# Beginning the products of two later recurrence units in the opening of a hybrid decoder trunk

## The chip, the cores and the metric

The kernel runs on one core of a Trainium2 chip, in one launch. The metric is the device time of that launch in microseconds (us). All shares, spans and waits below are from one execution that the hardware profiler recorded.

## The reference

Two layers over a stream of 256 tokens of width 2048, conditioned on a vector c. The first layer has two kinds of heads that share one input projection; the second has another linear attention. Cut to what matters here, the mixer of the first layer:

```python
def hgrn2_fox_mixer(h, w_in, w_out, lower_bound, a_out_gain, q_gain, k_gain, f_bias):
    proj = h @ w_in
    ...
    qa, fa, ia, ga, qb, kb, vb, gb, fb = jnp.split(proj, cuts, axis=-1)
    z = split_heads(fa, A_HEADS).astype(jnp.float32)
    ...
    o_a = chunk_gated_linear_recurrence(jax.nn.silu(split_heads(qa, A_HEADS)), key,
                                        split_heads(ia, A_HEADS), log_forget)
    o_a = rms_norm(o_a, a_out_gain[:, None, :])
    o_a = merge_heads(o_a).astype(h.dtype) * jax.nn.silu(ga)
    ...
    o_b = forgetting_attention(q, k, split_heads(vb, B_HEADS), log_f)
    o_b = merge_heads(o_b).astype(h.dtype) * jax.nn.sigmoid(gb)
    return jnp.concatenate([o_a, o_b], axis=-1) @ w_out
```

The input h is the normalised stream, shifted and scaled by vectors that are products of silu(c) with a matrix `mod_w`. All of it is float32.

## The kernel before

**Products.** A product is 256 tokens by 1024 columns over 2048 rows of a weight matrix, or 16 k tiles of 128 rows. To keep float32 accuracy both operands are split into a rounded high half and the rest: ScalarE casts the weights to `hi` (L167), VectorE takes `lo = raw - hi` (L169), and TensorE makes three matmuls of 128x512 for each block (L190 to L192: hi·hi, hi·lo, lo·hi). A load brings 1 MiB, which is two *pieces* of two k tiles for one product of 512 columns; a piece is 12 matmuls. A product's sum (`acc`, 128 x 2 x 512) lies in one of the two buffers of the PSUM pool `pp`.

**Units.** The first layer's projection is cut into four recurrence units A0 to A3 and four attention units B0 to B3, each of two heads and two products (A20, A21 and so on). The products of A0 and A1 are made in the opening, the others in the body.

**The opening** (`start()`, L962 to L1135) is an order written out by hand. For each of 16 k tiles SP issues three loads of 1 MiB: two column tiles of `mod_w` (L984) and one tile of `start_w` (L989), which holds the 2048 columns of A0 and A1. VectorE sums the two column tiles (L109), ScalarE and VectorE make that k tile's operand hT (L1015 to L1017), and TensorE does 24 matmuls (L1031 to L1033), or, for the k tiles in `PLAIN`, 8 float32 matmuls without splitting (L1026). Three raw weight tiles, four `hi` and four `lo` buffers go round.

**The body** (`drive()`, L222) walks a list of pieces: first A2, A3, then B0 to B3, then the output projection O0 and what follows. Between pieces it issues steps of *jobs*. A job is a unit's recurrence (`hgrn_scores`: exponents ex, decays dec, products kd, scores sc, the state st; `hgrn_output`: output po, its squares oj, o) or its attention. `TICKS` gives each job a number of pieces within which it is to be done, and `finish` forces what is left before the next unit of its kind goes on. Column sums for later modulation (L109) are spread over the pieces at a rate for each product. From this program a scheduler fixes each engine's order, and the buffer that each tile gets; on the chip every engine runs its list strictly in order. An attention unit's second product is read by the copy of v (L792) and by the gate g_B: three functions on ScalarE (L294 to L296) and L794 on VectorE, which releases the sum's buffer.

Of the kernel before, what the change touches and what calls it, by code (L numbers as in the profile page):

```python
# [7 lines left out]
F32 = mybir.dt.float32  # L8
# [16 lines left out]
PLAIN = (0, 3, 6, 9, 12, 15)  # L25
# [6 lines left out]
TICKS = dict(hgrn0=12, hgrn1=19, hgrn=14, fox_gates=6, fox_probs=6, fox_out=6,  # L32
# [34 lines left out]
def build(tc, ctx, a, out):  # L67
# [74 lines left out]
    def add(name, w, act, done, before=None, rate=0.0, first=False, last=False):  # L142
        p = Product(name, w, act, done, before, rate)
        p.first, p.last = first, last
        pieces.extend((p, k) for k in range(2 * len(w)))
# [31 lines left out]
    def multiply(i, tiles=(0, 1)):  # L177
# [5 lines left out]
        for kk in range(2):  # L183
# [3 lines left out]
            for t in tiles:  # L187
                a_hi, a_lo = p.act(kt, t)
                o = p.ps[:, t, :]
                nc.tensor.matmul(o, a_hi, w_hi, start=(kt == 0), stop=False)  # L190
# [771 lines left out]
    def start():  # L962
# [15 lines left out]
        def fetch_columns(kt):  # L978
            for part in (1, 0):
                if (2 * kt + 1 - part) % 3 == 2:  # L980
# [6 lines left out]
        def fetch_weights(kt):  # L987
            raw_w[kt] = rawp.tile([P, 2048], F32, tag="raw", name=f"raw_s{kt}")
            nc.sync.dma_start(out=raw_w[kt], in_=a["start_w"][kt])  # L989
# [12 lines left out]
        def weights(kt):  # L1002
            if kt in PLAIN:
                return None
            return [split_weights(raw_w[kt][:, n * 1024:(n + 1) * 1024], f"s{kt}_{n}") for n in range(2)]
# [13 lines left out]
        def products(kt, ws, ns):  # L1019

            for n in ns:
                sl = slice((n % 2) * 512, (n % 2 + 1) * 512)
                for t in range(2):
                    o = acc[n][t]
                    if ws is None:
                        nc.tensor.matmul(o, tms[kt][:, t * P:(t + 1) * P], raw_w[kt][:, n * 512:(n + 1) * 512],  # L1026
                                         start=(kt == 0), stop=(kt == KT - 1))
                        continue
# [4 lines left out]
                    nc.tensor.matmul(o, a_lo, hi[:, sl], start=False, stop=(kt == KT - 1))  # L1033
# [21 lines left out]
        acc = {}  # L1055
        env["pp"] = ctx.enter_context(tc.tile_pool(name="pp", bufs=2, space=PSUM))
        for u in range(2):
            big = acc["qg", u] = env["pp"].tile([P, 2, 512], F32, tag="pp", name=f"acc_s{u}")
            acc[2 * u + 1] = [big[:, t] for t in range(2)]
# [30 lines left out]
        for u in range(2):  # L1090
            acc[2 * u] = [ps_mix(f"acc_s{u}_{t}") for t in range(2)]
# [3 lines left out]
        operand(1)  # L1095
        fetch_columns(2)
        for kt in range(1, KT):
            if kt + 2 < KT:
                fetch_columns(kt + 2)
            if kt + 1 < KT:  # L1100
                fetch_weights(kt + 1)
                columns(kt + 1)
            if kt == 3:
                nc.scalar.preload_act_table_set(SILU)
            ws = weights(kt)
            if kt + 1 < KT:
                operand(kt + 1)
            products(kt, ws, (1, 3, 0, 2))
# [20 lines left out]
    def after_start(acc, qg):  # L1129
# [4 lines left out]
        for u in range(2):  # L1134
            env["last", u] = job(hgrn_scores(u, 0) + hgrn_scores(u, 1) + hgrn_output(u), TICKS[f"hgrn{u}"])  # L1135


    def done_hgrn(u, half):
        def done(ps):
            if half == 0:  # L1140
                finish(env["last", u - 2])
                urgent.extend(hgrn_gates(u, [(slice(0, 2), ps)]))
            else:
                assert not urgent
                env["A", u]["qg"] = hgrn_silu(u, ps)
                env["last", u] = job(hgrn_scores(u, 0) + hgrn_scores(u, 1) + hgrn_output(u), TICKS["hgrn"])
        return done

    def done_fox(u, half):
        def done(ps):  # L1150
            if half == 0:
                finish(env["last", u + 2])
# [4 lines left out]
            else:  # L1157
                fox_values(u, ps)
                env["last", u + 4] = job(fox_output(u) + ([lambda: end_mix("out_b")] if u == 3 else []), TICKS["fox_out"])
# [136 lines left out]
    for u in (2, 3):  # L1296
        for half in range(2):
            add(f"A{u}{half}", quads(a["ab_w_in"][2 * u + half]), now_act, done_hgrn(u, half), rate=RATES["A"])
    for u in range(4):
        for half in range(2):  # L1300
# [58 lines left out]
def _layout(i):  # L1359
# [18 lines left out]
    s = np.stack([w[:, g] for g in groups[:4]])  # L1378
# [40 lines left out]
```

## Time and profile before

| | us |
|---|---|
| median of 3 runs | 2499.93 (2498.66 to 2501.02) |
| the profiled execution | 2495.23 |
| its span, first to last instruction | 2493.50 |
| TensorE (PE) busy | 2442.0 (98%) |
| VectorE (DVE) busy | 1772.8 (71%) |
| ScalarE (ACT) busy | 1168.8 (47%) |

The mean granted clock of TensorE is 0.997. A group's row gives line, engine, operation, output and inputs, shapes and count, then busy time and the mean of one in ns, then the idle time before it and what ended that. A wait's row gives the engine and work that waited, what it waited for, the total, the number of times and the longest. In the chain each row is start, length and work.

### The profile page before, as it was taken

What the parts mean: (1) busy time and instruction counts of PE and PEld (TensorE: products, weight loads), DVE (VectorE), ACT (ScalarE), POOL (GpSimd) and SP (SyncE); (2) the same over time, 40 slices, a digit from 0 to 9 for tenths busy, and PEclk for the clock granted to TensorE, in tenths of its full rate; (3) what the DMA queues carried; (4) which work ended last, traced back from release to release, by engine and by line L of the source; (5) the groups of instructions that cost most, each with busy time, mean ns of one, the idle gap of its engine ahead of it and who ended that gap; (6) DMA issues with size and microseconds to landing.
All of it is one profiled execution on the core that took longest, in us unless ns stands there. A gap on an engine that the chain in (4) does not pass through costs nothing.

```text
span 2493.5 us, 28661 instructions
## 1 busy us (share of the span) xinstructions
PE 2442.0 (98%) x11204; PEld 2002.5 (80%) x11204; DVE 1772.8 (71%) x2039; ACT 1168.8 (47%) x1625; POOL 89.6 (4%) x176
## 2 busy tenths in 40 slices
PE   7899999999999999999999999999999999999999
PEld 4578887887888888888888888888888888888887
DVE  6967887887788767767767787876776554644555
ACT  4255555545434444344345666654544344344343
POOL 0000000000000000000000000000000000000000
PEclk9999999999999999999999999999999999999999
DMA  9964767985798877777786667677486555555554
GB/s 390 420 258 168 286 253 290 347 320 215 288 367 339 318 285 285 289 286 283 286 292 208 236 246 248 250 280 260 175 313 237 188 195 189 188 191 193 190 189 148
DMA packets 93849, 647.48 MB, mean 260 GB/s; under 512 B 10417, under 2 KB 10993, under 8 KB 16401
## 3 DMA queue, kind: packets, MB, share of 16 engines
q1 hardware_dynamic: 70290, 476.59, 52.4%
q0 software_dynamic: 23424, 169.07, 18.2%
q8 instruction: 87, 1.43, 0.2%
q14 instruction: 48, 0.39, 0.0%
HBM read 641.39 MB, written 4.23 MB: 259 GB/s over the span
## 4 chain that ended last, share of the span: by engine, by line
PE 93%; DVE 4%; DMA 2%; ACT 1%; issue 1%; SPq 0%; ACTq 0%
PE acc_F L192 13%; PE acc_F L190 13%; PE acc_F L191 13%; PE acc_G L190 6%; PE acc_G L192 6%; PE acc_G L191 6%; PE acc_C L192 4%; PE acc_C L190 4%; PE acc_C L191 4%; PE acc_B L190 2%; PE acc_B L192 2%; PE acc_B L191 2%; PE acc_O L190 2%; PE acc_O L192 2%; PE acc_O L191 2%; DMA raw_s<-in_start_w_dram 2%
## 5 line engine op out<-in xcount | busy, mean ns | idle before, releaser
L169 DVE TENSOR_TENSOR lo<-raw_F,hi 128x1024 fp32r<-128x1024 f32 x352 | 429.5, 1223 | 302.3 <-ACT hi L167 302.1
L167 ACT CAST hi<-raw_F 128x1024 fp32r<-128x1024 f32 x352 | 370.6, 1054 | 478.1 <-PE acc_F L192 433.2
L192 PE MATMUL acc_F<-hi,hT_f 128*128 128x512 f32 x1408 | 551.1, 391 | 1.4 <-DVE hT_f L357 1.4
L190 PE MATMUL acc_F<-hi,hT_f 128*128 128x512 f32 x1408 | 548.7, 390 | 1.8 <-ACT hT_f L356 1.8
L191 PE MATMUL acc_F<-lo,hT_f 128*128 128x512 f32 x1408 | 548.4, 390 | 0.0
L109 DVE SCALAR_TENSOR_TENSOR mod<-mod,silu_c 128x2048 f32<-128x2048 f32 x160 | 365.3, 2284 | 4.2 <-DMA mod<-in_mod_w_dram 4.2
L169 DVE TENSOR_TENSOR lo<-raw_G,hi 128x1024 fp32r<-128x1024 f32 x176 | 214.2, 1222 | 139.3 <-ACT hi L167 139.1
L167 ACT CAST hi<-raw_G 128x1024 fp32r<-128x1024 f32 x176 | 185.4, 1055 | 268.5 <-PE acc_G L192 227.3
L192 PEld LDWEIGHTS acc_F<-hi,hT_f 128*128 128x128 f32 x1408 | 264.4, 188 | 56.9 <-DVE hT_f L357 3.0
L190 PEld LDWEIGHTS acc_F<-hi,hT_f 128*128 128x128 f32 x1408 | 264.5, 188 | 55.8 <-ACT hT_f L356 2.2
L191 PEld LDWEIGHTS acc_F<-lo,hT_f 128*128 128x128 f32 x1408 | 264.3, 188 | 55.1
L190 PE MATMUL acc_G<-hi,ct_f 128*128 128x512 f32 x704 | 273.5, 389 | 1.6 <-DVE res_G L405 1.6
L192 PE MATMUL acc_G<-hi,ct_f 128*128 128x512 f32 x704 | 274.4, 390 | 0.0
L191 PE MATMUL acc_G<-lo,ct_f 128*128 128x512 f32 x704 | 273.7, 389 | 0.0
L190 PEld LDWEIGHTS acc_G<-hi,ct_f 128*128 128x128 f32 x704 | 132.2, 188 | 29.6 <-DVE res_G L405 2.4
L191 PEld LDWEIGHTS acc_G<-lo,ct_f 128*128 128x128 f32 x704 | 132.2, 188 | 27.4
L192 PEld LDWEIGHTS acc_G<-hi,ct_f 128*128 128x128 f32 x704 | 132.2, 188 | 27.2
L190 PE MATMUL acc_C<-hi,hT_n 128*128 128x512 f32 x384 | 152.4, 399 | 0.9 <-ACT hT_n L356 0.9
L192 PE MATMUL acc_C<-hi,hT_n 128*128 128x512 f32 x384 | 151.3, 394 | 0.7 <-DVE hT_n L357 0.7
L191 PE MATMUL acc_C<-lo,hT_n 128*128 128x512 f32 x384 | 151.7, 395 | 0.0
L104 POOL DMA_DIRECT2D mod<-in_mod_w_dram x160 | 84.5, 528 | 1612.8 <-DVE mod L109 1449.8
L169 DVE TENSOR_TENSOR lo<-raw_C,hi 128x1024 fp32r<-128x1024 f32 x96 | 116.1, 1220 | 35.2 <-ACT hi L167 34.8
(343 smaller groups left out, 3399.7 us busy)
## 6 DMA issues: line engine op xcount, KB each, us to landing
raw_F<-in_ffn_w_in_dram SPq DMA_DIRECT2D x176, 1024.0 KB, 4.9
mod<-in_mod_w_dram POOLq DMA_DIRECT2D x160, 1024.0 KB, 5.2
raw_G<-in_ffn_w_out_dram SPq DMA_DIRECT2D x88, 1024.0 KB, 4.9
raw_C<-in_gla_w_in_dram SPq DMA_DIRECT2D x48, 1024.0 KB, 5.6
mod_s<-in_mod_w_dram SPq DMA_DIRECT2D x32, 1024.0 KB, 17.0
raw_B<-in_ab_w_in_dram SPq DMA_DIRECT2D x32, 1024.0 KB, 6.6
raw_s<-in_start_w_dram SPq DMA_DIRECT2D x16, 1024.0 KB, 13.9
raw_A<-in_ab_w_in_dram SPq DMA_DIRECT2D x16, 1024.0 KB, 5.0
```

The source lines that it names most:

```text
L104: nc.gpsimd.dma_start(out=tile, in_=a["mod_w"][l, part * KT + j])
L109: nc.vector.scalar_tensor_tensor(tile, tile, 1.0, silu_c, ALU.mult, ALU.mult, accum_out=modc[l, part][:, j:j + 1])
L167: nc.scalar.copy(out=hi, in_=w)
L169: env["lo"] = nc.vector.tensor_tensor(lo, w, hi, ALU.subtract)
L190: nc.tensor.matmul(o, a_hi, w_hi, start=(kt == 0), stop=False)
L191: nc.tensor.matmul(o, a_hi, w_lo, start=False, stop=False)
L192: nc.tensor.matmul(o, a_lo, w_hi, start=False, stop=(kt == last))
```

## The change

The opening gets four steps ahead of its 16: ("e", 0) to ("e", 3) multiply the first four k tiles with the 2048 columns of A2 and A3, from a new array `early_w` of 4 MiB, into the sums that A0 and A1 use afterwards. Eight ScalarE copies of 128x512 take these partial sums to two tiles in SBUF, and the accumulators are allotted anew. The column sums of k tiles 0 to 3 go with the four new steps, so steps s0 to s3 have none. The plain steps are now five of twenty: e0, s5, s8, s11 and s15 (before: 0, 3, 6, 9, 12 and 15 of sixteen). The column tiles of part 0 always take the two `modraw` buffers, those of part 1 the pool `h`; before, one in three took `modraw`.

In the body the products of A2 and A3 begin at their third piece, and a VectorE add puts the saved sums on (once for each of four products). Their order is A0 A1 B0 A2 B1 A3 B2 B3, and `finish` goes by the unit two places ahead in that order. The deadlines of A0 and A1 go from 12 to 9 and from 19 to 16.

```diff
-PLAIN = (0, 3, 6, 9, 12, 15)
+EARLY = 4
+PLAIN = (("e", 0), ("s", 5), ("s", 8), ("s", 11), ("s", 15))
+ORDER_AB = (("A", 0), ("A", 1), ("B", 0), ("A", 2), ("B", 1), ("A", 3), ("B", 2), ("B", 3))
...
-TICKS = dict(hgrn0=12, hgrn1=19, hgrn=14, fox_gates=6, fox_probs=6, fox_out=6,
+TICKS = dict(hgrn0=9, hgrn1=16, hgrn=14, fox_gates=6, fox_probs=6, fox_out=6,
...
-        pieces.extend((p, k) for k in range(2 * len(w)))
+        p.begin = begin
+        pieces.extend((p, k) for k in range(begin, 2 * len(w)))
...
-                if (2 * kt + 1 - part) % 3 == 2:
+                if part == 0:
                     tl = rawp.tile([P, D], F32, tag="modraw", name=f"mod_s{part}_{kt}", bufs=2)
...
+        steps = [("e", kt) for kt in range(EARLY)] + [("s", kt) for kt in range(KT)]
+        new = [kt if g == "e" or kt >= EARLY else None for g, kt in steps]
...
+        for i in range(len(steps)):
+            if i + 2 < len(steps) and i > 0 and new[i + 2] is not None:
+                fetch_columns(new[i + 2])
+            if i + 1 < len(steps):
+                if i > 0:
+                    fetch_weights(i + 1)
+                if i > 0 and new[i + 1] is not None:
+                    columns(new[i + 1])
...
+            if i > 0:
+                products(i, ws, (1, 3, 0, 2))
+            if i == EARLY - 1:
+                for u in range(2):
+                    early[u] = hpool.tile([P, 2, 2, 512], F32, tag="h", name=f"early_{u}")
+                for half in (1, 0):
+                    for u in range(2):
+                        for t in range(2):
+                            nc.scalar.copy(out=early[u][:, half, t], in_=acc[2 * u + half][t])
+                wide("s")
+                narrow("s")
...
     def done_hgrn(u, half):
         def done(ps):
+            nc.vector.tensor_tensor(ps, ps, env["early"][u - 2][:, half], ALU.add)
             if half == 0:
-                finish(env["last", u - 2])
+                finish(env["last", before_last("A", u)])
...
-    for u in (2, 3):
+    for kind, u in ORDER_AB[2:]:
         for half in range(2):
-            add(f"A{u}{half}", quads(a["ab_w_in"][2 * u + half]), now_act, done_hgrn(u, half), rate=RATES["A"])
-    for u in range(4):
-        for half in range(2):
+            if kind == "A":
+                add(f"A{u}{half}", quads(a["ab_w_in"][2 * u + half]), now_act, done_hgrn(u, half), rate=RATES["A"], begin=EARLY // 2)
+                continue
```

Three places where the engines' lists differ follow. Rows read line, operation, output, inputs and shape; the numbers in names tell one tile from another.

*VectorE in the opening*, behind the column sums of k tile 3 (`mod_s` is a column tile, `lo_s` a lo half, `raw_se` a tile of early_w, `raw_ss` one of start_w). Before:

```order
L169 TENSOR_TENSOR lo_s_0_328<-raw_s_275,hi_s_0_327 128x1024
L169 TENSOR_TENSOR lo_s_1_332<-raw_s_275,hi_s_1_331 128x1024
L1017 TENSOR_TENSOR hT_s_194<-tm_s_335,hT_s_194 128x256
L109 SCALAR_TENSOR_TENSOR mod_s_4_317,modc_1_83<-mod_s_4_317,silu_c 128x2048
L109 SCALAR_TENSOR_TENSOR mod_s_4_319,modc_0_82<-mod_s_4_319,silu_c 128x2048
```

Now:

```order
L172 TENSOR_TENSOR lo_s_0_324<-raw_se_275,hi_s_0_323 128x1024
L172 TENSOR_TENSOR lo_s_1_328<-raw_se_275,hi_s_1_327 128x1024
L1025 TENSOR_TENSOR hT_s_194<-tm_s_331,hT_s_194 128x256
L172 TENSOR_TENSOR lo_s_0_362<-raw_se_317,hi_s_0_361 128x1024
L172 TENSOR_TENSOR lo_s_1_366<-raw_se_317,hi_s_1_365 128x1024
L172 TENSOR_TENSOR lo_s_0_413<-raw_ss_359,hi_s_0_412 128x1024
L172 TENSOR_TENSOR lo_s_1_417<-raw_ss_359,hi_s_1_416 128x1024
L172 TENSOR_TENSOR lo_s_0_447<-raw_ss_409,hi_s_0_446 128x1024
L172 TENSOR_TENSOR lo_s_1_451<-raw_ss_409,hi_s_1_450 128x1024
L172 TENSOR_TENSOR lo_s_0_485<-raw_ss_444,hi_s_0_484 128x1024
L172 TENSOR_TENSOR lo_s_1_489<-raw_ss_444,hi_s_1_488 128x1024
L111 SCALAR_TENSOR_TENSOR mod_s_4_478,modc_1_83<-mod_s_4_478,silu_c 128x2048
```

Eight lo halves, of steps e3, s0, s1 and s2, now stand between hT of k tile 3 and the column sums of k tile 4.

*TensorE around the second head of A0* (ex: exponents; sc, cx: scores; po: output). Before, inside the second product of A2 (`acc_A_1242`):

```order
L459 MATMUL ex_A_0_0_0_1045<-lvl,lf_A_861 128x512 x2
L190 MATMUL acc_A_1242<-hi_1236,hT_s_374 128x512
L191 MATMUL acc_A_1242<-lo_1237,hT_s_374 128x512
L192 MATMUL acc_A_1242<-hi_1236,hT_s_374 128x512
L190 MATMUL acc_A_1242<-hi_1236,hT_s_374 128x512
L191 MATMUL acc_A_1242<-lo_1237,hT_s_374 128x512
L192 MATMUL acc_A_1242<-hi_1236,hT_s_374 128x512
L459 MATMUL ex_A_0_0_1_1049<-lvl,lf_A_861 128x512 x2
L459 MATMUL ex_A_1_0_0_1054<-lvl,lf_A_861 128x512 x2
L190 MATMUL acc_A_1242<-hi_1274,hT_s_374 128x512
```

Now, from the last matmul of B01 (`acc_B_1498`) to the first of A20 (`acc_A_1887`), and on ScalarE the rows that end there:

```order
L195 MATMUL acc_B_1498<-hi_1742,hT_s_848 128x512
L462 MATMUL ex_A_0_0_0_1295<-lvl,lf_A_1037 128x512 x2
L462 MATMUL ex_A_0_0_1_1299<-lvl,lf_A_1037 128x512 x2
L462 MATMUL ex_A_1_0_0_1304<-lvl,lf_A_1037 128x512 x2
L462 MATMUL ex_A_1_0_1_1308<-lvl,lf_A_1037 128x512 x2
L518 MATMUL sc_A_1337<-dec_A_0_0_1294,kd_A_0_0_1312 128x64 x4
```

```order
L653 ACTIVATE oj_A_1418,hss_A_1405<-po_A_1407 128x128
L653 ACTIVATE oj_A_1420,hss_A_1405<-po_A_1407 128x128
L795 COPY v_B_1848<-acc_B_1498 128x512
L297 ACTIVATE g_B_1849<-acc_B_1498 128x512
L288 ACTIVATE rsu_A_1423<-rsm_A_1422 128x4
L298 ACTIVATE g_B_1849<-g_B_1849 128x512
L289 ACTIVATE hr_A_1406<-rsu_A_1423 128x4
L299 ACTIVATE g_B_1849<-g_B_1849 128x512
```

All of that head's small matmuls lie in a row behind B01 and ahead of A20, and the gate of B0, whose last step releases the buffer that A20 gets, stands on ScalarE behind that head's squares.

*VectorE at the end of A21* (picks: COPY_PREDICATED into the state st). Before, at the same step of A0's recurrence:

```order
L169 TENSOR_TENSOR lo_1409<-raw_A_3_1138,hi_1408 128x1024
L109 SCALAR_TENSOR_TENSOR mod_2_1_1424,modc_2_84<-mod_2_1_1424,silu_c 128x2048
L169 TENSOR_TENSOR lo_1437<-raw_A_0_1240,hi_1436 128x1024
L169 TENSOR_TENSOR lo_1474<-raw_A_0_1240,hi_1473 128x1024
L548 COPY_PREDICATED st_80<-lmask,sc_A_1087 128x8x16
```

Now, in A1's recurrence:

```order
L490 TENSOR_TENSOR dec_A_1_0_1646<-dec_A_1_0_1646,qkTs_A_0_1616 128x1024
L172 TENSOR_TENSOR lo_2151<-raw_B_1_2022,hi_2150 128x1024
L1173 TENSOR_TENSOR acc_A_2024<-acc_A_2024,early_393 128x1024
L172 TENSOR_TENSOR lo_2186<-raw_B_1_2022,hi_2185 128x1024
L111 SCALAR_TENSOR_TENSOR mod_2_10_2201,modc_2_84<-mod_2_10_2201,silu_c 128x2048
L551 COPY_PREDICATED st_80<-lmask,sc_A_1662 128x8x16
L551 COPY_PREDICATED st_80<-lmask,sc_A_1662 128x16x8
```

The add of the saved sums, which waits for A21's last matmul, now stands ahead of the picks.

74 lines of the change are left out of this document (39 added, 35 removed).

## The prediction

> **What bounds the kernel now.** I read the busy times and the chain of waits on the page first, then the windows, then the chain of the first 200 us.
>
> ```profile
> PE 2442.0 (98%) x11204; PEld 2002.5 (80%) x11204; DVE 1772.8 (71%) x2039; ACT 1168.8 (47%) x1625; POOL 89.6 (4%) x176
> PE 93%; DVE 4%; DMA 2%; ACT 1%; issue 1%; SPq 0%; ACTq 0%
> 0.00:147.60 147.60, 118.60 (x376) 72.24 (x376) 114.93 (x160) 55.00 (x85) 5.17 (x14) 0.97 0.97 392
> 147.60:560.00 412.40, 402.77 (x2053) 340.71 (x2054) 328.59 (x445) 228.14 (x466) 24.39 (x47) 1.00 0.73 272
> 40.00:60.00 20.00, 18.26 (x64) 11.89 (x64) 18.84 (x26) 7.56 (x11) 0.00 (x0) 1.00 1.01 419
> ```
>
> The columns of a window are its length, the busy time of PE, PEld, DVE, ACT and POOL, the granted clock, the DMA share and GB/s. TensorE is the bound: behind the opening it stands 412.40 − 402.77 = 9.6 us in the part that the change reorders. So a matmul taken out there is worth its full pitch, and a stall put in there costs its full length. The opening (0 to 147.6) is another matter:
>
> ```profile
> 41.32 0.34 DVE hT_s L1017
> 41.66 4.42 DVE mod_s L109 x4
> 46.28 2.28 DVE lo_s L169 x2
> 48.56 0.33 DVE hT_s L1017
> 48.89 4.42 DVE mod_s L109 x4
> 53.61 0.61 ACT tm_s L1015
> ...
> 55.10 4.42 DVE mod_s L109 x4
> ...
> 89.93 17.57 DMA raw_s<-in_start_w_dram
> ...
> 111.04 21.69 DMA raw_s<-in_start_w_dram
> 132.81 1.05 ACT hi_s L167
> ...
> 140.67 6.88 PE acc_s L1026 x16
> 147.58 1.03 ACT qg_A L1113
> ```
>
> These rows are start, length and work. Up to 89.93 the chain is VectorE's (two column sums L109, then the lo halves L169), from there the loads', with DMA at 1.01 of its time. TensorE has slack there, and the change puts work into that slack. But that work brings 4 MB of loads of its own.
>
> **The opening.** It moves 3 tiles of 1 MiB for each of 16 k tiles, and 2 MiB of x. A MiB at 419 GB/s takes 2.50 us. Four more tiles cost 4 × 2.50 = 10.0 us if the queue never pauses: the lower bound.
>
> The queue pauses, and so does VectorE. Steps e0 to e3 take the first four column tiles, steps s0 to s3 take none, so all four steps without column sums lie in a row, while 24 column sums stay to be done behind them. Up to 48.9 (hT of k tile 3) all goes as before. Then, by rows:
>
> ```profile
> L109 DVE SCALAR_TENSOR_TENSOR mod_s<-mod_s,silu_c 128x2048 f32<-128x2048 f32 x32 | 72.1, 2284 | 2.5 <-DMA mod_s<-in_mod_w_dram 2.5
> L1049 ACT COPY xT<-xT 128x512 f32<-128x512 f32 x8 | 4.5, 587 | 11.8 <-PE xT L1047 11.8
> 379.81 0.23 PE acc_B L190
> 384.11 0.23 PE acc_B L191
> ```
>
> The last two are the first and the 20th of an unbroken run of matmuls in the chain: 4.30 / 19 = 0.2263 us each, 5.4 us for a step of 24. A plain step takes 6.88. TensorE ends e3 at about 58.3. ScalarE copies the sums out (8 × 0.587, mostly under e3, to 59.1), loads its function table and begins the hi cast of s0 at 60.3. One hi cast and one lo half (1.05 and 1.14, half of L169's 2.28) later TensorE starts: s0 runs from about 62.5 to 68.0, s1, s2 and s3 5.4 us each behind it. The column sums of k tile 4 stand on VectorE behind the lo halves of s2, which want buffers that s0 holds: they begin at 70.3, not at 48.9. From there VectorE has 12 column tiles: nine with lo halves (41.66 to 48.89: 7.23) and three without (48.89 to 55.10: 6.21), 9 × 7.23 + 3 × 6.21 = 83.7 us, to 154.0. The first lo half of s14 is done by 152.4, so its 24 matmuls end about 157.9 and the plain s15, 6.88 later, at **164.8**. The load queue says nearly the same: with tiles at 2.50 us and pauses of some 6 us while three raw buffers wait for lo halves, the last split tile lands at 150, and 2.4 (hi, lo) + 5.4 + 6.88 behind that is 164.7. So **+17.2** (bounds +10.0, and +21 if sums and loads wait for each other for half a step).
>
> **The products.** A2 and A3 (four products of half a unit) lose 2 of 8 pieces: 4 × 2 × 12 = 96 matmuls, × 0.2263 = **−21.7**. Eight hi casts, eight lo halves and 4 MB go too: worth nothing where PE bounds. The four adds (128x1024 from PSUM) have a nearest row of 1222 ns.
>
> **Waits that go or come.** An accumulator has two buffers, and a product can begin only when the last reader of the buffer it gets is done. This is what that costs now:
>
> ```profile
> PE acc_B L190 <- DVE g_B L794: 4.3, 2, 4.1
> PE acc_A L190 <- ACT v_A L584: 1.5, 1, 1.5
> 380.00:400.00 20.00, 15.93 (x71) 12.88 (x70) 14.12 (x23) 12.83 (x43) 1.37 (x3) 0.91 0.70 268
> 387.85 2.29 DVE mod L109 x2
> 391.43 0.61 DVE g_B L794
> 392.08 0.55 PE acc_B L190
> 392.63 0.43 PE acc_B L191
> 395.99 0.23 PE acc_B L190
> ```
>
> At 388.0 B11 ends; its gate (copy, Abs, Exp, Ln on ScalarE, L794 on VectorE) takes 4.0 us, and the next product waits 4.1. Behind that wait eight matmuls come at 0.43 instead of 0.23: **1.6 us** more, at a granted clock of 0.91. Both waits lie at boundaries that the new order does away with: 4.1 + 1.6 + 1.5 = **−7.2** (bounds −9.6, −4).
>
> The new order puts A and B units in turn, and in the program of the change three boundaries have such a chain, longer each time. The durations:
>
> ```profile
> L460 ACT ACTIVATE dec_A<-ex_A 128x512 f32<-128x512 f32 x32 | 18.0, 598 | 9.6 <-PE ex_A L459 9.5
> L487 DVE TENSOR_TENSOR dec_A<-dec_A,qkTs_A 128x1024 f32<-128x1024 f32 x8 | 9.7, 1218 | 0.0
> L487 DVE TENSOR_TENSOR kd_A<-dec_A,qkTs_A 128x384 f32<-128x384 f32 x16 | 8.3, 551 | 0.0
> L548 DVE COPY_PREDICATED st<-lmask,sc_A 128x128 f32<-128x128 int32 x40 | 14.2, 355 | 4.8 <-ACT st L540 3.8
> L401 DVE TENSOR_TENSOR res_O<-acc_O,gate 128x1024 f32<-128x1024 f32 x2 | 2.4, 1222 | 2.8 <-PE acc_O L192 2.8
> ```
>
> *B01 to A20.* The first matmul of A20 waits for the gate of B0. That gate stands on ScalarE and VectorE behind the whole second head of A0's recurrence, which before ran between the matmuls of A21. From the end of B01: about 1.5 us until the first exponent matmuls may start, four of dec (2.4, the first under the matmuls), the multiplies behind them (1.09, 0.55 × 2, 1.09, 1.22 = 4.5), scores and state copies 1.4, six picks 2.1, outputs and their squares 1.3, then copy, Abs, Exp, Ln and L794 3.6: about 16 us, in which TensorE has 31 small matmuls, 4.5 us. **+11.5** (bounds 4.1, the longest such wait now, and 14).
>
> *A21 to B10.* The buffer is released by a copy on ScalarE behind A1's output, that behind the picks, and these on VectorE behind the add (1.22), a lo half (1.22) and a column sum (2.28), all after A21's last matmul: 4.7 + 2.1 + 2.0 = 8.8, less 1.8 of small matmuls: **+7.0** (bounds 1.5 and 8.8).
>
> *B31 to O0.* The gate of B3, 4.0 as at 388, with eight squares (0.25 apart, 2.0) and three casts (1.0) of other jobs between on ScalarE: 7.0, less 2.5 of small matmuls: **+4.5** (bounds 0 and 7).
>
> Each is over the 4.1 us that brought the slow matmuls: 3 × 1.6 = **+4.8** (bounds 0, and 23.0 × 1.6 / 4.1 = 9.0 if the slow stretch grows with the wait; I take the row as it stands, since none longer is seen).
>
> The Trainium skill, "TensorE: Matmul & The Clock Gate", part 1 on the HAM clock gate, states that an idle window of about 3.4 us drops the array to half clock and that about 3.4 us of work bring it back, however long the idleness was. The trace's eight matmuls of 0.43 agree with its 3.4 us. By the rule three long waits cost one such ramp each, and the sum would be as it stands below; if the slow stretch grew with the wait, it would be 4.2 higher.
>
> **The sum** against the profiled execution, whose own time is 2495.23 (span 2493.50): 17.2 − 21.7 − 7.2 + 11.5 + 7.0 + 4.5 + 4.8 = **+16.1**, 2511.3. The median of the runs shown is 4.7 above the profiled one, so **2516** for a median.
>
> **Rivals.** *The gain is kept (faster).* VectorE and the queue catch up, so the opening costs only +10, and ScalarE is far enough ahead that the three waits stay near what the boundaries cost now (7.2, for 7.2 gone): 10 − 21.7 = −11.7, 2488. For it: ScalarE is busy 228 of 412 us here, and no boundary now costs over 4.1. Against: the three chains start at a product's last matmul, so being ahead doesn't shorten the last two.
>
> *They cancel.* The opening as forecast, but A20's wait is small, because A0's second head runs earlier: 16.1 − 11.5 − 1.6 = +3, 2503. For it: the largest term rests on where VectorE stands when B01 ends. Against: the exponent matmuls stand behind B01's last matmul in the program.
>
> *Slower still.* Behind a long wait ScalarE has squares and scales of B0 (16 small ones, 5.5 us) ahead of the next hi cast; from the fifth half piece on (10.9 us) TensorE would wait for casts, some 4 us at two of the boundaries, with the opening at +21: +28, 2528. Four hi buffers speak against it.
>
> *The moved work is hidden only in part*, the opening as forecast and the new waits equal to the old: 17.2 − 21.7 = −4.5, 2495. It lies between the first two, and shares their chances.
>
> **Chances.** Forecast (2508 to 2524) 0.46; slower still 0.12; cancel or nearly (2495 to 2508) 0.20; gain kept 0.22. A measurement here tells 0.2%, 5 us, from no change. Of the gain kept 0.20 is over that, of the cancel case 0.06 on the slow side: faster 0.20, same 0.16, slower 0.64. The likeliest case alone spans 2508 to 2524; down to the gain kept and up to half of the last case, the range is 2490 to 2526.
>
> **What would show it.** The last x16 group of acc_s should end near 165 and the first column sum of k tile 4 start near 70; near 158 means that the queue bounds. TensorE's waits should list acc_A behind g_B at about 11.5, acc_B behind v_A at about 7, acc_O behind g_B at about 4.5, with slower matmuls after each. If none of them is over 4 us, the forecast is wrong, and the first rival holds. If the opening ends before 155, both its workings are wrong.

## The result, and the profile after

The changed kernel takes 2534.7 us (median of 4, 2531.7 to 2535.2) against 2499.3 (median of 4, 2495.2 to 2501.0) for the kernel before: a ratio of 1.0142, with a 95% interval of 1.0124 to 1.0159. The forecast of 2516 had the sign and less than half of the size, and the time lies outside its range of 2490 to 2526.

The page of the changed kernel, busy times and the shares of the chain:

```profile
PE 2458.5 (97%) x11212; PEld 2018.6 (80%) x11212; DVE 1779.3 (70%) x2045; ACT 1175.9 (46%) x1635; POOL 89.6 (4%) x176
PE 91%; DVE 5%; DMA 2%; ACT 1%; issue 0%; SPq 0%; ACTq 0%; DVEq 0%
```

The time goes by stages. The windows of the kernel before, cut at the end of the opening, the first matmul of the body, the first of O0 and the first behind O0 (columns: from and to, length, busy time of PE, PEld, DVE, ACT, POOL with the number of records, granted clock, DMA share, GB/s):

```profile
0.00:147.58 147.58, 118.60 (x376) 72.24 (x376) 114.93 (x160) 54.98 (x85) 5.17 (x14) 0.97 0.97 392
148.65:496.24 347.59, 340.48 (x1746) 288.69 (x1747) 279.17 (x383) 195.93 (x415) 20.69 (x40) 1.00 0.71 262
496.24:601.14 104.90, 101.75 (x497) 84.78 (x495) 80.20 (x101) 51.06 (x79) 5.28 (x10) 1.00 0.79 303
601.14:2493.50 1892.36, 1881.17 (x8587) 1556.75 (x8587) 1298.45 (x1397) 865.78 (x1046) 58.47 (x112) 1.00 0.68 246
```

The same windows of the changed kernel:

```profile
0.00:173.08 173.08, 141.06 (x480) 93.65 (x480) 126.44 (x170) 69.33 (x102) 5.16 (x14) 0.96 0.91 361
174.16:518.79 344.63, 326.04 (x1642) 276.74 (x1643) 274.52 (x375) 187.02 (x398) 20.68 (x40) 0.96 0.69 255
518.79:640.79 122.00, 110.19 (x503) 91.25 (x504) 79.81 (x105) 51.87 (x89) 5.27 (x10) 0.91 0.67 249
640.79:2533.10 1892.31, 1881.18 (x8587) 1556.91 (x8587) 1298.41 (x1397) 866.62 (x1046) 58.50 (x112) 1.00 0.68 246
```

The opening is 25.5 us longer, the units A and B 3.0 shorter, O0 17.1 longer, and the rest is the same to 0.1 us. That adds up to the 39.6 between the two spans. The execution profiled before is the fastest of its four and none of the four after took longer than the one profiled, so the spans lie 39.6 apart and the medians only 35.4. The reader should look at the second row twice: TensorE is busy 14.4 us less in the units, but stands 18.6 us instead of 7.1. And in the third row, in a product that the change doesn't touch, it is busy 8.4 us more and stands 8.7 more.

**The opening.** From its chain of waits (start, length, work), the rows where it changes hands:

```profile
40.59 0.80 PE acc_e L1042
41.38 0.43 PE acc_e L1043
63.98 0.79 PE acc_s L1042
73.20 4.42 DVE mod_s L111 x4
126.19 11.61 DMA mod_s<-in_mod_w_dram
140.57 16.12 DMA raw_ss<-in_start_w_dram
159.13 0.80 PE acc_s L1042
166.18 6.88 PE acc_s L1036 x16
```

VectorE carries the chain from 73.2 to 126.2, then the loads carry it to 156.7, and cast, lo half, 24 matmuls and a plain step follow. The first matmul behind each wait takes 0.79 or 0.80 and the next ones 0.43, where 0.23 is usual: they run at half clock. Six windows show where the queue loses time:

```profile
30.00:40.00 10.00, 5.28 (x20) 2.51 (x18) 5.66 (x8) 6.00 (x10) 0.00 (x0) 0.98 0.93 368
40.00:50.00 10.00, 9.41 (x29) 7.57 (x30) 10.00 (x13) 5.35 (x8) 0.00 (x0) 0.68 0.48 165
50.00:60.00 10.00, 9.69 (x43) 7.70 (x41) 1.51 (x2) 3.98 (x8) 0.00 (x0) 1.00 0.95 383
60.00:70.00 10.00, 6.53 (x21) 5.06 (x22) 4.63 (x4) 5.95 (x7) 0.00 (x0) 0.83 0.45 168
70.00:80.00 10.00, 10.00 (x46) 8.28 (x45) 9.25 (x10) 4.75 (x6) 0.00 (x0) 1.00 0.99 405
80.00:90.00 10.00, 10.00 (x46) 8.29 (x45) 10.00 (x14) 3.13 (x4) 0.00 (x0) 1.00 0.96 368
```

The DMA share is 0.48 and 0.45 in two of them, while the steps without column loads run and the three raw buffers are full (SP waits up to 12.1 us for a lo half before it issues a load of `start_w`). By the shares, 10.7 us of the queue's time are lost in these two and 12.4 in all six, and what it still has to bring lands later for it.

**The units.** TensorE's longest waits from 150 to 620 us (total, times, longest):

```profile
PE pT_B L784 <- ACT s_B L778: 8.9, 1, 8.9
PE po_A L561 <- DVE st L551: 4.2, 1, 4.2
PE acc_A L193 <- DVE g_B L797: 3.9, 1, 3.9
PE sc_A L518 <- DVE dec_A L490: 3.6, 1, 3.6
PE acc_O L193 <- DVE g_B L797: 2.5, 1, 2.5
```

The three boundaries of the forecast are all there: dec_A and g_B ahead of A20, st ahead of B10, g_B ahead of O0. What they cost beside the idle time shows in the windows of the small matmuls ahead of A20 and of its first matmuls:

```profile
234.20:244.20 10.00, 8.87 (x40) 8.61 (x40) 3.55 (x8) 1.21 (x7) 0.00 (x0) 0.50 0.17 72
249.43:254.43 5.00, 5.00 (x12) 3.94 (x13) 1.56 (x8) 3.69 (x22) 0.00 (x0) 0.50 0.00 0
```

The clock is at 0.50 in both: 12 matmuls fill 5 us, and the scores, whose results the next wait needs, run at half speed too. From B01's end (229.4) to A20 (249.4) it takes 20.0 us.

**O0.** The longest wait of all lies in it, and the forecast had nothing there. The timeline of TensorE, ScalarE, VectorE and SP's queue there:

```profile
567.78 0.28 PE L767 MATMUL sc_B<-tri,nlf_lo 128*128 128x128 f32 x1
576.93 0.47 PE L784 MATMUL pT_B<-ident,s_B 128*128 128x128 f32 x1 [8.87 <-ACT s_B L778]
...
569.85 1.99 ACT L170 CAST hi<-raw_O 128x1024 fp32r<-128x1024 f32 x2 [7.09 <-DMA raw_O<-in_ab_w_out_dram]
...
570.93 1.23 DVE L172 TENSOR_TENSOR lo<-raw_O,hi 128x1024 fp32r<-128x1024 f32 x1 [8.01 <-ACT hi L170]
572.07 2.29 DVE L111 SCALAR_TENSOR_TENSOR mod<-mod,silu_c 128x2048 f32<-128x2048 f32 x1
574.28 1.22 DVE L172 TENSOR_TENSOR lo<-raw_O,hi 128x1024 fp32r<-128x1024 f32 x1
575.42 0.74 DVE L776 SCALAR_TENSOR_TENSOR s_B<-sc_B,fcol,cmask 128x128 f32<-128x128 f32 x2
...
551.69 1.97 SPq L416 DMA_DIRECT2D xold<-in_x_dram  x4
553.77 9.51 SPq L163 DMA_DIRECT2D raw_O<-in_ab_w_out_dram  x3
```

At 567.8 the scores of B3's second head are done. Their masking on VectorE (L776) stands in order behind two lo halves and a column sum, and the first of these waits for a weight tile that lands at 569.8, because 3 MiB of gate and old x were issued ahead of it. The transposes wait for all of that, 8.9 us, with no weight matmul in between. The same two rows of TensorE in the kernel before:

```profile
536.32 0.28 PE L764 MATMUL sc_B<-tri,nlf_lo 128*128 128x128 f32 x1
541.96 0.28 PE L781 MATMUL pT_B<-ident,s_B 128*128 128x128 f32 x1
```

They lie 5.6 us apart, and TensorE doesn't stand at all: 24 weight matmuls of O0 lie between. Behind the wait the change pays once more:

```profile
576.93:589.93 13.00, 11.74 (x36) 9.14 (x37) 2.58 (x7) 2.00 (x5) 0.00 (x0) 0.53 0.35 147
```

Thirteen us at a granted clock of 0.53.

### The profile page after: what moved, and what is told of

It reads as the page before. It is cut to its first block, busy times and chain, and to the rows that moved or that the text cites. A ratio compares the mean times of both kernels' runs of the same rounds, so it can differ in the third digit from the quotient of the medians.

```text
span 2533.1 us, 28703 instructions
## 1 busy us (share of the span) xinstructions
PE 2458.5 (97%) x11212; PEld 2018.6 (80%) x11212; DVE 1779.3 (70%) x2045; ACT 1175.9 (46%) x1635; POOL 89.6 (4%) x176
## 4 chain that ended last, share of the span: by engine, by line
PE 91%; DVE 5%; DMA 2%; ACT 1%; issue 0%; SPq 0%; ACTq 0%; DVEq 0%
PE acc_F L195 13%; PE acc_F L194 13%; PE acc_F L193 13%; PE acc_G L193 6%; PE acc_G L194 6%; PE acc_G L195 6%; PE acc_C L195 3%; PE acc_C L193 3%; PE acc_C L194 3%; PE acc_B L193 2%; PE acc_B L195 2%; PE acc_B L194 2%; PE acc_O L193 2%; PE acc_O L194 2%; PE acc_O L195 2%; DVE mod_s L111 2%
## 6 DMA issues: line engine op xcount, KB each, us to landing
mod_s<-in_mod_w_dram SPq DMA_DIRECT2D x32, 1024.0 KB, 11.7
```

## The experiments

All were timed beside the kernel before, on one chip for each group, and a ratio is to the runs of the kernel before in that group (medians 2497.9 to 2499.3). The stages come from each profile: the first matmul of the body, the length of the units, of O0 and of the rest (us). A profiled execution can lie up to 6.5 us from its kernel's median (e10), so stages and medians needn't add up.

| kernel | body from | units | O0 | rest | median | ratio and 95% interval |
|---|---|---|---|---|---|---|
| before | 148.7 | 347.6 | 104.9 | 1892.4 | 2499.3 | |
| the change | 174.2 | 344.6 | 122.0 | 1892.3 | 2534.7 | 1.0142 (1.0124 to 1.0159) |
| e1 old order | 174.5 | 347.2 | 119.2 | 1892.3 | 2534.6 | 1.0148 (1.0133 to 1.0164) |
| e2 order only | 147.9 | 353.2 | 107.5 | 1895.7 | 2504.6 | 1.0026 (1.0015 to 1.0037) |
| e3 columns earlier | 171.5 | 343.6 | 120.1 | 1892.4 | 2530.5 | 1.0132 (1.0117 to 1.0147) |
| e4 gate line early | 172.8 | 345.0 | 115.9 | 1895.5 | 2530.8 | 1.0132 (1.0115 to 1.0149) |
| e5 fewer sums in O0 | 172.7 | 345.7 | 113.1 | 1894.2 | 2530.8 | 1.0135 (1.0118 to 1.0152) |
| e6 columns even | 164.4 | 345.2 | 122.2 | 1892.3 | 2527.9 | 1.0120 (1.0105 to 1.0135) |
| e7 two early tiles | 161.2 | 347.9 | 118.8 | 1892.4 | 2522.7 | 1.0102 (1.0087 to 1.0117) |
| e8 = e4 + e5 + e6 | 168.6 | 346.7 | 112.9 | 1894.1 | 2523.7 | 1.0102 (1.0087 to 1.0118) |
| e9 filled waits | 172.7 | 347.1 | 117.9 | 1895.6 | 2532.9 | 1.0135 (1.0118 to 1.0152) |
| e10 two tiles, even, filled | 154.6 | 353.0 | 119.8 | 1893.8 | 2516.5 | 1.0079 (1.0064 to 1.0094) |
| e11 four tiles, even, filled | 164.9 | 344.3 | 113.2 | 1895.6 | 2519.7 | 1.0085 (1.0070 to 1.0100) |
| e12 scores ahead | 174.1 | 343.0 | 115.9 | 1895.5 | 2531.5 | 1.0130 (1.0115 to 1.0146) |
| e13 = e5 + e12 | 174.7 | 346.5 | 113.8 | 1894.0 | 2529.8 | 1.0123 (1.0106 to 1.0140) |
| e14 = e5 + e6 + e12 | 167.1 | 345.3 | 113.8 | 1894.3 | 2522.1 | 1.0094 (1.0079 to 1.0109) |

The opening of one and the same order varies by up to 4 us between profiles (e6, e11, e14, e8: 164.4, 164.9, 167.1, 168.6), so a difference under that in a single pair of profiles says nothing. Of the whole time, the change loses 35.4 us to the kernel before, e3, e4, e5 and e12 lose 32.6 to 33.1 and e6 29.9. The intervals of these, of e1, e9 and e13 overlap that of the change, so what their edits do is read from the stages alone; with early steps, only e7, e8, e10, e11 and e14 are clear of the change in the whole time.

### Is it the order of the units? (e1, e2)

```diff
-ORDER_AB = (("A", 0), ("A", 1), ("B", 0), ("A", 2), ("B", 1), ("A", 3), ("B", 2), ("B", 3))
+ORDER_AB = (("A", 0), ("A", 1), ("A", 2), ("A", 3), ("B", 0), ("B", 1), ("B", 2), ("B", 3))
```

> Only the order of units is put back (A0 A1 A2 A3 B0 B1 B2 B3); the opening, the add and the deadlines stay as in the change. First theory (the trace of the change: opening +25.5, units A and B -2.9, output projection O0 +17.1): the opening ends at 173 as in the change, the units take 21.7 us less than before with waits of some 7 us as before, so +4 over before if O0's pause belongs to the order, +21 if not. Rival (the order is the whole cost, the opening only looks long): below before, -5 or less.

With the early products kept and the old order put back, nothing is won: 2534.6 is 36.7 over the kernel before, where the dearer reading had 21. The old order doesn't bring its old waits back, but others, by TensorE's waits in e1:

```profile
PE acc_B L193 <- DVE g_B L797: 11.4, 2, 7.5
```

and O0 keeps a wait of 8.7 for s_B. So the pause in O0 isn't the order's.

e2 is the other half: the kernel before with the new order and the new deadlines, no early steps.

```diff
+ORDER_AB = (("A", 0), ("A", 1), ("B", 0), ("A", 2), ("B", 1), ("A", 3), ("B", 2), ("B", 3))
-TICKS = dict(hgrn0=12, hgrn1=19, ...
+TICKS = dict(hgrn0=9, hgrn1=16, ...
```

> Only the alternate order and the deadlines 9 and 16 are put into the kernel before; no early steps, all 8 pieces in the body. First theory: opening 147.6 as before, units A and B +12 to +19 by the new waits, O0 0 to +17: +12 to +36 over before. Rival (the waits come from the add and the shorter products, not from the order): within 5 us of before.

It costs 0.26%, 6.7 us, between what its theory and its rival had. The units take 5.6 us more, and nearly all of it is clock, by the windows of e2 (all units; B01 to A20):

```profile
147.90:501.10 353.20, 345.56 (x1739) 293.14 (x1739) 279.03 (x382) 195.31 (x412) 20.82 (x40) 0.97 0.70 257
207.90:227.90 20.00, 14.94 (x57) 13.38 (x58) 6.61 (x21) 7.79 (x38) 0.00 (x0) 0.51 0.01 3
```

TensorE is busy 5.1 us more with the same work and idle 0.5 more. (The 3.3 that its rest is longer are clock as well; see below.) The order alone is a small loss, and the change's large loss needs the early steps.

### What bounds the opening? (e3, e6, e7)

e3 takes the column loads and sums of k tiles 4 to 15 three steps earlier, one k tile in each step:

```diff
+            early_kt = i + 1 if i > 2 else (new[i + 2] if i > 0 else None)
+            if early_kt is not None and early_kt < KT and (i > 2 or early_kt < EARLY):
+                fetch_columns(early_kt)
...
+                elif i > 3 and i < KT:
+                    columns(i)
```

> The change, but loads and column sums of k tiles 4 to 15 come three steps earlier, one in each of the steps s0 to s11, and none in s12 to s15; the operands stay where they were. First theory (four steps without column sums in a row leave VectorE and the load queue idle, and the 24 sums behind them are the bound): opening ends near 158 instead of 173, 13 to 17 us less than the change. Rival (54 MiB of loads bound the opening whatever the order): 168 or later, at most 5 us less.

e6 lays them evenly over s0 to s14, three steps with and one without:

```diff
+        spread = dict(zip((4, 5, 6, 8, 9, 10, 12, 13, 14, 16, 17, 18), range(4, 16)))
...
+            if i + 1 in spread:
+                fetch_columns(spread[i + 1])
...
+                if i in spread:
+                    columns(spread[i])
```

> The change with one edit in the opening: the column sums of k tiles 4 to 15 and their loads, which follow one another in steps s3 to s14, are laid evenly over steps s0 to s14, three steps with and one without. Theory (gap): the opening's excess is the queue's lost time where four steps have no column loads; spread evenly, 54 MiB at 2.50 us run without a gap, raw tiles come in step, and the opening ends at 158 to 163 instead of 173.1, the time at 2520 to 2525. Rival (coupling): VectorE, the three raw buffers and TensorE hold each other up in each step, whatever the order; the opening stays at 168 to 174 (170.5 with the sums three steps earlier), the time at 2529 to 2536.

e3 wins 2.6 us of the opening only, less than the spread. Its chain shows why it isn't more: with the column loads ahead of them the raw weights come last, the tile of s11 lands at 140.0, and TensorE then runs 30.4 us without a pause to the end at 170.5. e6 ends the opening at 163.3, 9.8 earlier. Its window at 60 and the last loads in its chain:

```profile
60.00:70.00 10.00, 8.20 (x23) 6.19 (x24) 8.69 (x10) 4.88 (x6) 0.00 (x0) 0.66 1.00 407
...
118.86 11.81 DMA raw_ss<-in_start_w_dram
134.21 12.68 DMA raw_ss<-in_start_w_dram
156.43 6.88 PE acc_s L1036 x16
```

The share is 1.00 where it was 0.45, and the last load lands at 146.9 instead of 156.7. But e6 has the shortest of the four openings of this order: they begin the body at 166.3 in the mean, and the seven profiles with the opening of the change (172.7 to 174.7) at 173.7. So about 7.4 of the 25.5 us, not 9.8, were the gap; the median falls by 6.8, 3 less than was expected at least. Of the 15.8 that e6 still costs, 10.0 are four more tiles, some 4 are queue time still lost (DMA shares of 0.81 to 0.96 in four of its windows between 30 and 110), and the rest stands behind the last tile, slow matmuls included.

```diff
-EARLY = 4
+EARLY = 2
...
-        fetch_columns(2)
+        if new[2] is not None:
+            fetch_columns(2)
```

> The change with two early k tiles in place of four: 2 MiB less in the opening, two steps without column sums instead of four, and 48 matmuls fewer taken out of the products of A2 and A3 instead of 96. If each early k tile costs the same (25.5 / 4 = 6.4 us), the opening ends at 160.3, the products are 10.9 longer than in the change, and the time stays within 3 us of the change if O0's pause is as there, 2533. If the cost is in the row of steps without column sums (it grows faster than their number), the opening ends at 152 to 156; with the products, 2525 to 2530 with O0's pause of 17 and 2510 to 2515 without.

Two early tiles cost 12.5 us of opening, just half of the change's 25.5. The guess that the cost grows faster than the number of steps without sums falls: it is in proportion. Its units are 3.3 longer than the change's, where 48 matmuls (10.9 us) came back. TensorE stands 2.9 less in them; the other 4.7 are busy time, and part of that is only moved, as O0 has 19 more records there than in the change.

### Where do O0's 17 us come from? (e4, e5, e12, e13)

e4 writes the gate's line one unit earlier; e5 mixes fewer column sums into O0:

```diff
-                if u == 3:
+                if u == 2:
                     gate_line(0, 2)
```

```diff
-RATES = dict(A=0.3, B=1.05, O0=0.8, F0=0.5, C=0.5, O1=0.4, F1=0.4)
+RATES = dict(A=0.3, B=1.25, O0=0.4, F0=0.5, C=0.5, O1=0.4, F1=0.4)
```

> The change, but the line of the first output gate is written out when the first product of B2 is done, not of B3. First theory (SyncE's queue stands at that line's store and then at the load that needs it, so the next raw tile of O0 comes late): the wait of 8.9 us in O0 and the slow matmuls behind it go, 12 to 17 us less than the change. Rival (the 3 MiB of the old stream and the gate row ahead of that raw tile are what delays it): 0 to 4 us less.

> The change with one edit: the rate at which column sums of later blocks (1 MiB load and 2.28 us of VectorE each) are mixed into the output product O0 goes from 0.8 to 0.4 for each weight tile, and that of the B units from 1.05 to 1.25, so that as many are done by the end (6.4 leave O0, 6.4 more lie in the B units). Theory (the queue): during O0 a weight tile of 5.4 us of matmuls brings 1.8 MiB with its column loads, of the 2.16 MiB that the queue can move, so the 3 MiB of gate and old x can't be caught up and the weight tile behind them lands late. With 1.4 MiB instead it is caught up: the wait for s_B of 8.7 falls under 3, O0 takes 107 to 110 instead of 122, the units stay at 344 to 348, and the time is 2519 to 2524. Rival (the order of issue): the tile is late because it stands behind the gate line's landing on SP, whatever else is loaded; O0 stays at 118 to 123 and the time at 2531 to 2538.

The transposes in e4, and in e5:

```profile
570.70 0.39 PE L784 MATMUL pT_B<-ident,s_B 128*128 128x128 f32 x1 [3.88 <-ACT s_B L778]
```

```profile
572.23 0.33 PE L784 MATMUL pT_B<-ident,s_B 128*128 128x128 f32 x1 [2.44 <-ACT s_B L778]
```

In e4 the tile lands earlier, but a column sum still stands ahead of the masking, and 3.9 remain. In e5 the tile is there and the sum gone, and 2.4 remain: one lo half, then the bare chain from the scores through masking, maximum and exponent. e5's wait is as expected (under 3), but O0 comes to 113.1, not to 110, and the median lies at 2530.8, 7 above the top of what was expected. e4's median is 3.9 under the change's, which is its rival's number, though the wait fell by 5.0 and O0 by 6.1: 3.2 of that came back in the rest. Nor do the two add up: e8 with both has O0 at 112.9. And a short wait alone doesn't make O0 short: in e7 the transposes wait 2.6, and O0 still takes 118.8, with TensorE busy 112.1.

e12 therefore puts back the order of TensorE in the kernel before, with the loads as late as in the change:

```diff
+        after = env["scores"].ins if p.name == "O0_1" and k == 5 else None
...
-                nc.tensor.matmul(o, a_hi, w_hi, start=(kt == 2 * p.begin), stop=False)
+                with tc.issue_after(after) if after is not None else ExitStack():
+                    nc.tensor.matmul(o, a_hi, w_hi, start=(kt == 2 * p.begin), stop=False)
```

> The change with one edit in the order of TensorE: the last 24 weight matmuls of O0 that don't need B3 (its second output block, pieces 5 and 6) stand behind the scores of B3's second head, as in the kernel before, and no more ahead of them. Loads and sums are as in the change. Theory (cover): before, 24 matmuls (5.4 us) lie between these scores and the transposes that wait for their softmax, in the change none; with them back the wait pT_B for s_B falls from 8.9 to under 3.5, some of it going to the qkTs copies ahead of the scores (1.2), O0 takes 110 to 116 instead of 122, and the time is 2523 to 2529. Rival (late load): the weight tile that lands 51 us into O0 holds TensorE up wherever the scores stand; the wait shows under another name (acc_O behind lo) with 6 us or more, O0 stays at 118 or over, the time at 2530 or over.

> The same edit together with fewer column loads in O0 (0.4 a tile, 1.25 in the B units). Alone, the fewer loads left a wait of 2.4 of the transposes for the softmax, with nothing between. Theory (cover): that wait goes too, O0 takes 107 to 111 against 113.1, the time is 2525 to 2529. Rival: O0 is no shorter than 113 because the wait moves to the copies ahead of the scores.

In e12 the wait of 8.9 is gone, and its rest shows in other places, two of them here by TensorE's timeline:

```profile
560.57 0.49 PE L762 MATMUL sc_B<-qkTs_B 128*128 128x128 f32 x2 [1.17 <-ACT qkTs_B L752]
...
570.84 0.49 PE L813 MATMUL po_B<-v_B,pTs_B 128*128 128x128 f32 x2 [2.19 <-ACT pTs_B L788]
```

The second stands behind the late tile again: the copy of the transposed probabilities follows that tile's cast on ScalarE. Two more waits, 1.5 and 0.9, are for o_B behind it. O0 takes 115.9 instead of 122.0, the upper end of what the cover would give, and the median of 2531.5 lies 2.5 over it. So three different edits (line, sums, order) each take 6 to 9 us off, and together no more than 9: they are three links of one chain, and with any one of them shortened the next bounds. e13 shows the floor again, 113.8, no better than e5 without the cover; 1.1 of it now lies ahead of the scores, as its rival had it. Of what is left over the kernel before, some 8 us, the windows give 3.2 to slow weight matmuls in e5 (92.8 busy on the 384 weight matmuls, 89.7 before), and 2.4 to idle time; the remaining 2.6 go with 24 more records of small work that now lies behind O0's first matmul.

### Is the slow clock worth buying off? (e9)

```diff
+    def warm(ps, n, w=512):
+        for _ in range(n):
+            last = nc.tensor.matmul(ps, lvl[:, :P], lvl[:, :w], start=True, stop=True)
+        return last
...
+            if (u, h) == (0, 1):
+                warm(b0, 14)
...
+            if (u, h) == (3, 1):
+                warm(pt, 30)
```

> The change with matmuls of constants, whose results nothing reads, put into four waits of TensorE: 14 of 128x512 ahead of the scores of A0's second head (idle 3.6 before), 60 of 128x128 ahead of A20 (3.9), 30 of 128x256 ahead of A1's last output (4.2) and 30 of 128x512 ahead of the late transposes in O0 (8.9). Nothing that the waits wait for is changed. Theory (clock): the halved clock behind a wait comes from the idle time alone, so the granted clock stays near 1.00 in these places: the 12 matmuls behind A20's wait, the 8 behind B10's and the scores between go from 0.43 to 0.23 and half, some 8 us in the units, and O0's 12.5 us at half clock become 6.3; 2533 less 14 gives 2519 to 2524. Rival: the fillers only take the place of the idle time, because the slow stretch has another cause or because the chain that is waited for sets the next start anyway; 2530 to 2538.

The clock does what was expected ahead of A20 and behind it, by the windows of e9, and at the end of O0's wait it does not:

```profile
238.00:248.26 10.26, 8.74 (x77) 8.65 (x77) 3.85 (x14) 7.02 (x33) 0.00 (x0) 1.00 0.01 2
248.26:253.26 5.00, 5.00 (x24) 4.14 (x24) 1.37 (x5) 4.38 (x15) 0.00 (x0) 1.00 0.00 0
577.00:585.00 8.00, 6.74 (x21) 4.87 (x21) 1.81 (x5) 1.06 (x2) 0.00 (x0) 0.58 0.51 213
```

There are 24 records in the 5 us behind A20's first matmul, where the change has 12. But A20 starts 75.5 us after the body's first matmul, in the change 75.3. The clock did win something: with the scores at full clock, L816 (the change's L797), which frees A20's buffer, is done 71.5 us after the body's first matmul instead of 75.1. The 60 small fillers, 0.11 each and 6.9 us together, stood ahead of A20 and took these 3.6 back. A wait of 4.2 for st, like the change's ahead of B10, now lies ahead of a later unit (at 399.1). Nothing is won, 2532.9. So at A20 the full clock is worth 3.6 us, and the fillers ate it. That it would be worth 14 in all is neither shown nor excluded: the fillers were put in by guess, and too many of them.

### What is left when the repairs go together (e8, e10, e11, e14)

These join the edits above; e10 and e11 have the fillers (with 10 in O0), e10 two early tiles.

> Three edits of the change at once: column sums spread evenly in the opening, fewer column loads in O0 (0.4 instead of 0.8 per tile, 1.25 in the B units), and the gate line of O0 written one unit earlier. If the opening's gap and O0's queue are the two causes, their gains add: opening 158 to 163, units 344 to 348, O0 105 to 109, the time 2504 to 2511, still over the kernel before. If neither is the cause, 2527 to 2535.

> All that has helped so far with two early k tiles: column sums spread evenly over the opening's 18 steps, column loads in O0 at 0.4 a tile (1.25 in the B units), fillers ahead of A0's second head (14), A20 (60 small) and O0's late transposes (10). If the causes are those found, the opening ends at 154 to 157 (two tiles at the 3.9 us that each costs when spread evenly), the units take 341 to 346, O0 107 to 111, the rest 1894: 2500 to 2508, no better than the kernel before. If two tiles cost 12.5 in the opening whatever the order, 2508 to 2514.

> The same with four early k tiles (and the filler of A1's last output). Opening 163 to 167, units 335 to 340 because the moved 21.7 us are now cut by less idle and less slow time, O0 106 to 110: 2502 to 2511. If it stands at or under the version with two early k tiles, the early work pays its own way once the waits are cheap; if it is 4 us or more over it, each early tile costs more in the opening than it saves behind it.

> The repairs that hold, together, with four early k tiles: column sums spread evenly in the opening, fewer column loads in O0, scores ahead of the last free weight matmuls. Opening 163 to 168, units 344 to 347, O0 106 to 111, rest 1894: 2509 to 2517 for a median, so that the change stays slower than before by 10 or more, the opening's 16 to 20 against 3 won in the units. At or under 2503 something in this account is wrong.

All come out over what was expected: 2523.7, 2516.5, 2519.7, 2522.1. In e8 and e14 the opening is at the long end of its spread, and O0 stays near 113 where under 111 was expected. In e10 the opening costs only 5.9 us for two tiles, less than expected, but its units take 353.0, 5.4 more than before with 48 matmuls fewer. Against e7, the other version with two tiles, they are 5.1 longer: TensorE stands 2.7 less (though 5.5 and 3.8 for st and g_B ahead of O0) and is busy 7.8 more, and the fillers alone are 10.7. Whether two or four early tiles are better with all repairs stays open (2516.5 and 2519.7, a difference inside the spread of their runs). No version with early steps comes to the kernel before; the best still loses 0.8%.

## Why the prediction was wrong

| step | forecast | measured |
|---|---|---|
| opening | +17.2 (10 to 21) | +25.5 |
| units up to O0's first matmul | −2.7 | −3.0 |
| O0 | +1.6 | +17.1 |
| rest | 0 | −0.1 |
| sum | +16.1 | +39.6 |

The forecast missed 23.5 us of the 39.6. Of these 15.5 are O0's, where it had next to nothing, and 8.3 the opening's, where a term was too small; the units came out right by luck.

**The opening: the mechanism right, one term too small.** The first column sum of k tile 4 started at 73.2, against 70.3, and the last sum ended at 156.0, against 154.0; that side of the working holds. The step that failed is "pauses of some 6 us" in the load queue's side: the six windows above give 12.4, and the last split tile landed at 156.7 instead of 150, and the 14.7 behind it became 16.3, because 8 matmuls of s14 ran at half clock. 6.7 + 1.6 = 8.3 is the whole miss. The bound of +21 was too low as well, since VectorE and the queue were taken as alternatives: each says nearly the same, so one was thought to confirm the other, while in truth VectorE bounds to 126 and the queue, already late, from there on. The evenly spread openings, most of the gap closed, end at 163.3 to 167.5, about the 164.7 of the forecast's queue.

**The units: the right sum of wrong parts.** The products gave their −21.7. Of the three new waits, A20's was to stand 11.5 and stands 8.4 (3.6 + 0.9 + 3.9), B10's 7.0 and 5.4 (4.2 + 1.2), O0's 4.5 and 4.8 (1.4 + 0.9 + 2.5). Idle time is thus 11.5 up, not 17.4. But busy time fell only 14.4 of the 21.7: slow matmuls cost 7.3 where the forecast had 1.6 more than before in the units (two of its three ramps, less the one that went). The step "3 × 1.6 = **+4.8**" is the wrong one: eight matmuls of 0.43 behind each wait, as at 388. It priced only the weight matmuls behind the wait, and left out the 40 small ones inside it, which also ran at 0.50 and lie on the chain that the wait is for. The small work was undercounted too: from B01's end to A20 the forecast had 31 small matmuls and 4.5 us, and the trace has 54 records, busy 11.7 us of 20.0. That A20's idle time came out under the forecast is thus no sign of a shorter chain: it is 20.0 us long, and was to be 16.

**The clock.** No length of wait decides in these traces whether the clock halves. A wait of 2.4 us left it at 1.00 in e5, one of 2.6 halved it in e7 and one of 2.8 in e2, and a run of short ones (none over 0.7, e9 at 577 to 585) halved it too. The rest, where all kernels do the same work, shows it best. At three places of it a new xT has been made and the next product begins, and there TensorE waits 0.9 and then 0.7 us in every profile. In the change it goes on at 1.00; in e4 eight matmuls follow at 0.43, at two of the three (635 and 1376), and each such stretch costs 1.6. The rests of 1892.3, of about 1894 and of about 1895.6 in the table have none, one and two of them, with the same waits throughout. The slow stretch was 1.6 us of loss at 388 before, 12 matmuls (5.0 us long) behind A20's wait, and 13 us behind O0's, where two short waits of 0.6 and 0.7 fall into it. The Trainium skill, "TensorE: Matmul & The Clock Gate", part 1 on the HAM clock gate, gives about 3.4 us of sustained work for the ramp. The eight matmuls at 388 (3.4 us) agree with it; A20's 5.0 us are half as long again, behind O0's wait the stretch is nearly four times as long, and the measurement decides. One ramp for each wait was too little; that small matmuls which wait for one another don't end the ramp would fit the rows, but was not tested by itself.

**O0: not looked at.** The forecast followed the new order to O0's first matmul and stopped there. Yet its own sources would have told more: in the order of TensorE in the changed program, the last scores of B3 stand directly ahead of the transposes that need them, where before 24 weight matmuls lie between. From the profile of before the price could have been had: the weight tile's cast at 540.1 waited 3.7 us for its load, with TensorE covered by those very matmuls. O0 had no slack before. e12 shows that the cover is worth 6 us of O0, e5 and e4 that the late tile and the column sum ahead of the masking are the rest of the same chain. Why the scheduler puts the scores 24 matmuls later in the change is not settled: e1, with the old order, has it too, e2, with the new order and no early steps, has 11 matmuls between and a wait of 1.5.

**The rivals.** "The gain is kept" and "they cancel" both fell with the opening, which alone cost more than the products gave. "Slower still" had the sign and 2528, but not the cause: no cast is waited for behind the new waits. The opening's end at 155 or 158, named as signs, was passed by 15 us or more.

## What to carry to other kernels

Work moved under a bound that is "not TensorE" wasn't free here, because it brought loads of its own: each early 1 MiB tile saved 5.4 us and cost 6.3 in the opening (3 to 5 with the column loads spread), and new waits took the rest. When loads of two kinds share a queue, lay them out evenly: the stretch without column loads was queue time that this opening didn't get back. And when an edit moves the time at which a later stage starts, read the order in that later stage as well: whatever separates a chain's two ends there, here 24 matmuls of cover, is part of the price.

## What the runs showed that was not expected

- Three repairs of one wait don't add: 122.0 for O0 fell to 115.9, 113.1 and 115.9 by one edit each, and to 112.9 and 113.8 by two.
- Filling TensorE's waits with idle work restores the clock (0.50 to 1.00 around A20) and wins nothing (2532.9 against 2534.7): A20's buffer was free 3.6 us earlier, and the fillers, 6.9 us long there, stood in the way.
- Gaps of 0.57 and 0.68 us one behind the other leave the clock at 1.00 in the kernel before and in e5, and it is at 0.50 through the same gaps in the change and in e9. There, something else came shortly before; in the rest of the change and of e4 even that is the same, and the clock still differs. What decides it isn't settled.
